# A row-sum kernel: closing barriers under the last store, and another order of waits

## The chip, the cores and the metric

The kernel runs on one core of a Trainium2 chip. The time is device microseconds (us) of one execution. Beside it stands the span: from the first to the last instruction of the program in the profile. The time is longer than the span; the difference is called the *rest* here.

A ratio is the mean time of one kernel's fast runs over that of the kernel before in the same rounds, so not quite the ratio of the medians quoted beside it. Spans of single runs are known to 0.1 us; a mean rest over four or five runs is therefore good to about 0.03 us.

## The reference

```python
batch, seq, dim = 32, 512, 1024          # x: float32, 64 MiB
def reference(x, divisor):               # divisor = 1024.0
    return (np.sum(x, axis=-1) / divisor).astype(np.float32)
```

That is 16,384 rows of 1,024 numbers, each summed and divided.

## The kernel before

Each of the 128 partitions holds 128 rows. SyncE (SP) issues large loads, three buffers in turn. VectorE (DVE) sums most rows of a buffer in one reduction, and ScalarE (ACT) takes some. The last eight rows per partition come in ever smaller pieces; the last row is cut into `pa`, `pb` and `pc`, so that little work is left when the last bytes land. Of the kernel's body only the end is shown here; the comments are added:

```python
    load(pa, x_last[:, L - 1, :a])
    load(pb, x_last[:, L - 1, a:b])
    load(pc[:, : D - b], x_last[:, L - 1, b:])

    nc.gpsimd.tensor_scalar_mul(out=res, in0=res, scalar1=scale)
    tc.keep_in_program_order(nc.sync.dma_start(out=o_main, in_=res))     # 60 KB

    act_sum(pc[:, D - b : D - b + 1], pa)
    nc.vector.reduce_sum(out=pc[:, D - b + 1 :], in_=pb, axis=AX)        # L124
    nc.vector.reduce_sum(out=q[:, L - 1 :], in_=pc, axis=AX)             # L125
    nc.vector.scalar_tensor_tensor(out=fin, in0=q, scalar=scale, in1=r, op0=MULT, op1=ADD)   # L126
    tc.keep_in_program_order(nc.sync.dma_start(out=o_last, in_=fin))     # L127, 4 KB
```

Behind this the framework closes the program (L158 in the profile). Two words for what follows: a *semaphore* is a counter that instructions and transfers change and that an instruction can wait on; a *drain* is an instruction of an engine's sequencer with which, here, an engine closes its work and joins a barrier. SyncE waits for everything that is still under way, the last store included. Then all five engines meet in a first barrier, GpSimd clears the program's semaphores, and they meet in a second barrier.

## Time and profile before

| what | before |
|---|---|
| time, median of 3 runs | 162.98 us |
| span of the profiled run | 161.5 us |
| last piece of input landed | 158.25 us |
| last arithmetic (L126) ended | 159.14 us |
| last store issued / landed | 159.17 / 160.58 us |
| last engine left the second barrier | 161.51 us |

Read it from below: the span ends 3.26 us after the last input byte, and nearly 2.4 us of that lie behind the last arithmetic. The change is about those microseconds alone. To the same end belongs this line of the closing records (duration in ns as min/median/max, first and last start), for the semaphore instructions of SyncE that start between 159.55 and 160.7 us:

```profile
L158 SPq EVENT_SEMAPHORE  x5: 27/28/912, 159.6 to 160.7; - x5
```

Four of the five take 28 ns or less. The fifth, 912 ns, holds the wait for the store to land.

### The profile page before, as it was taken

To read this page: it belongs to the slowest core of one execution; us is meant where nothing else is said; L and a number is where in the kernel's file an instruction comes from. 1 tells how busy PE (TensorE), PEld (TensorE's weight loads), DVE (VectorE), ACT (ScalarE), POOL (GpSimd) and SP (SyncE) were. 2 spreads that over 40 slices of the span, in tenths; PEclk is the share of its full clock that TensorE was granted. 3 is DMA by queue.
4 is the path that set the end of the run, shared out by engine and by line. 5 is a ranking of instruction groups with operands and counts; after the bars stand their busy time and mean duration, and the time that the engine had idled before them with its cause. 6 is when DMAs were issued, how large, how long until landed. Compare 5 with 4: busy or idle time off the path is not lost.

```text
span 161.5 us, 138 instructions
## 1 busy us (share of the span) xinstructions
DVE 120.0 (74%) x15; ACT 20.7 (13%) x39; POOL 0.8 (0%) x6
## 2 busy tenths in 40 slices
DVE  0000099968998699959995999599968970697893
ACT  3000000000000000000000000000008100682881
POOL 0000000000000000000000000000000000000100
DMA  9999999999989999999999899999999978999990
GB/s 298 398 440 454 454 454 454 454 440 440 412 355 398 454 454 454 454 454 454 440 440 412 355 398 454 454 454 454 454 454 440 440 327 383 487 414 394 410 384 6
DMA packets 2448, 67.18 MB, mean 416 GB/s; under 512 B 528, under 2 KB 912, under 8 KB 1040
## 3 DMA queue, kind: packets, MB, share of 16 engines
q1 hardware_dynamic: 2448, 67.18, 97.1%
HBM read 67.11 MB, written 0.07 MB: 416 GB/s over the span
## 4 chain that ended last, share of the span: by engine, by line
DMA 67%; DVE 29%; another core or an unknown queue 1%; SPq 1%; issue 0%; DVEq 0%
DMA t<-in_x_dram 45%; DVE res L87 28%; DMA row<-in_x_dram 22%; SPq L76 1%; DVE q L107 1%; DVE q L125 0%; DVE pc L124 0%; DVE fin L126 0%; DVEq L125 0%; DVEq L126 0%
## 5 line engine op out<-in xcount | busy, mean ns | idle before, releaser
L87 DVE TENSOR_REDUCE res<-t 128x14 f32<-128x14336 f32 (+3 forms) x9 | 114.4, 12716 | 38.2 <-DMA t<-in_x_dram 38.2
L81 ACT ACTIVATE junk<-t 128x1024 f32<-128x1024 f32 x17 | 17.2, 1013 | 135.6 <-DMA t<-in_x_dram 135.6
L87 DVE TENSOR_REDUCE q<-t 128x2 f32<-128x2048 f32 (+1 forms) x2 | 3.5, 1752 | 0.7 <-DMA t<-in_x_dram 0.7
L81 ACT ACTIVATION_READ_ACCUMULATOR junk<-t 128x1 f32 x17 | 3.2, 188 | 0.0
L81 ACT ACT_TABLE_LOAD x1 | 1.3, 1283 | 1.7 <-PEq L144 1.7
L120 POOL TENSOR_SCALAR res<-res 128x120 f32<-128x120 f32 x1 | 0.5, 513 | 151.0 <-DVE res L87 151.0
L107 DVE TENSOR_REDUCE q<-row 128x1 f32<-128x768 f32 x1 | 1.0, 953 | 0.1
L125 DVE TENSOR_REDUCE q<-pc 128x1 f32<-128x322 f32 x1 | 0.5, 489 | 0.1
L81 ACT ACTIVATE junk<-pa 128x448 f32<-128x448 f32 x1 | 0.5, 547 | 0.1
L124 DVE TENSOR_REDUCE pc<-pb 128x1 f32<-128x256 f32 x1 | 0.4, 420 | 0.0
L81 ACT ACTIVATE junk<-row 128x256 f32<-128x256 f32 x1 | 0.4, 388 | 0.2 <-DMA row<-in_x_dram 0.2
L126 DVE SCALAR_TENSOR_TENSOR fin<-q,r 128x8 f32<-128x8 f32 x1 | 0.2, 167 | 0.1
L81 ACT ACTIVATION_READ_ACCUMULATOR junk<-row 128x1 f32 x1 | 0.2, 188 | 0.0
L81 ACT ACTIVATION_READ_ACCUMULATOR junk<-pa 128x1 f32 x1 | 0.2, 185 | 0.0
L73 POOL MEMSET r<- 128x8 f32 x1 | 0.1, 105 | 1.3 <-POOLq L144 1.3
L144 POOL MEMSET const-bfloat16-1.0<- 128x1 bf16 x1 | 0.1, 102 | 0.0
L144 POOL MEMSET const-uint8-127<- 128x1 uint8 x1 | 0.1, 102 | 0.0
L144 POOL MEMSET const-float32-0.0<- 128x1 f32 x1 | 0.1, 99 | 0.2 <-issue 0.2
L144 POOL MEMSET const-float32-1.0<- 128x1 f32 x1 | 0.1, 100 | 0.0
## 6 DMA issues: line engine op xcount, KB each, us to landing
t<-in_x_dram SPq DMA_DIRECT2D x8, 7168.0 KB, 35.7
t<-in_x_dram SPq DMA_DIRECT2D x1, 4096.0 KB, 28.5
t<-in_x_dram SPq DMA_DIRECT2D x1, 2048.0 KB, 33.0
t<-in_x_dram SPq DMA_DIRECT2D x1, 1024.0 KB, 35.0
row<-in_x_dram SPq DMA_DIRECT2D x1, 512.0 KB, 35.9
pa<-in_x_dram SPq DMA_DIRECT2D x1, 224.0 KB, 36.0
pc<-in_x_dram SPq DMA_DIRECT2D x1, 160.0 KB, 35.7
pb<-in_x_dram SPq DMA_DIRECT2D x1, 128.0 KB, 35.8
```

What stands on the lines that cost most here:

```text
L73: nc.gpsimd.memset(r, 0.0)
L76: tc.keep_in_program_order(nc.sync.dma_start(out=dst, in_=src))
L81: nc.scalar.activation(junk[:, :n], src, COPY, scale=by, accum_out=dst)
L87: nc.vector.reduce_sum(out=dst[:, :d], in_=t[:, :d, :], axis=AX)
L107: nc.vector.reduce_sum(out=q[:, j : j + 1], in_=row[:, :c], axis=AX)
L120: nc.gpsimd.tensor_scalar_mul(out=res, in0=res, scalar1=scale)
L124: nc.vector.reduce_sum(out=pc[:, D - b + 1 :], in_=pb, axis=AX)
L125: nc.vector.reduce_sum(out=q[:, L - 1 :], in_=pc, axis=AX)
L126: nc.vector.scalar_tensor_tensor(out=fin, in0=q, scalar=scale, in1=r, op0=MULT, op1=ADD)
L144: nc = _bacc.Bacc("TRN2", target_bir_lowering=False, num_devices=1)
```

## The change

There are two parts. `close_while_storing` takes the last store out of the body and puts it behind SyncE's first closing drain, gives it a semaphore of its own (`landed`), and puts the wait for that semaphore behind both barriers. `latest_wait_first` sorts the waits of an instruction that has several. An instruction carries one wait itself (the *embedded* one, the first of the list); the others become separate semaphore instructions ahead of it on the engine's sequencer.

```diff
+def latest_wait_first(nc):
+    def rank(i, w):
+        own = {"DVE": "DVE_", "Activation": "Activation_", "SP": "DVE_", "Pool": "DVE_"}
+        if w.ant_name.startswith("DMAHW") and i.engine != SP:
+            return 0
+        return 1 if w.ant_name.startswith(own.get(str(i.engine).split(".")[-1], "?")) else 2
+    ...   # sorts on_wait of each body instruction by rank
+
+def close_while_storing(nc, landed):
+    ...   # drain: SyncE's first closing drain, without the waits for the store and for L126
+    last = nc.sync.wait_ge(landed, 16).ins
+    body.instructions = [i for i in body.instructions if i.name != store.name]
+    end.instructions = [
+        with_sync(drain, on_wait=tuple(needs.values())),
+        with_sync(store, on_wait=(done,), on_update=(add,)),
+        *end.instructions[1:-1],
+        with_sync(last, on_update=(sub,)),
+    ]
...
+    landed = nc.alloc_semaphore("landed")
     nc.at_finalize(start_loads_at_once)
+    nc.at_finalize(latest_wait_first)
+    nc.at_finalize(lambda nc: close_while_storing(nc, landed))
```

## The prediction

> **What bounds the kernel now.** I read the page first, for the limit of the bulk, then the chain of waits for the last microseconds, and then the records of the closing barrier, since the change touches only the end and the order of waits.
>
> The page's slices (the program's 161.5 us in 40 pieces; busy tenths of the DMA engines, and the rate):
>
> ```profile
> DMA  9999999999989999999999899999999978999990
> GB/s 298 398 440 454 454 454 454 454 440 440 412 355 398 454 454 454 454 454 454 440 440 412 355 398 454 454 454 454 454 454 440 440 327 383 487 414 394 410 384 6
> ```
>
> The 16 DMA engines are busy from the first slice to the last but one: the kernel reads 67.11 MB and is bound by that. The view by stretches says the same: from 10 to 120 us the DMA share is 1.00 at 434 GB/s, while VectorE is busy for 90.5 of those 110 us. The last piece of the input (`pc`) is issued at 122.52 and lands at 158.25 us by its record. Nothing before that can be moved by this change: it touches no load and no buffer.
>
> What follows is a serial tail. The chain of waits (start, us, what), its last lines:
>
> ```profile
> 121.04 35.86 DMA row<-in_x_dram
> 156.90 0.02 issue
> 156.93 0.95 DVE q L107
> 157.88 0.42 DVE pc L124
> 158.30 0.04 DVEq L125
> 158.33 0.05 issue
> 158.38 0.50 DVE q L125
> 158.88 0.03 issue
> 158.91 0.02 DVEq L126
> 158.93 0.04 issue
> 158.98 0.17 DVE fin L126
> ```
>
> The reader is to see two kinds of step. Between the landing of `row` and L107 there is 0.02 us: that wait is inside the instruction. Before L125 and L126 stands a `DVEq` piece with "issue" around it: a separate semaphore instruction on VectorE's sequencer waits first, and only then is the reduction handed to the engine. L124 to L125 costs 0.10 us so, and L125 to L126 0.10 us (158.87 to 158.98).
>
> The chain stops at the last arithmetic, 159.15 us; the span ends at 161.5. The missing 2.36 us are in SyncE's waits (us in total, times, longest), the issue table (KB, us to landing) and the records of the program's closing line (duration ns min/median/max, first and last start):
>
> ```profile
> SPq L158 <- DMA out_dram<-fin: 0.9, 1, 0.9
> SPq L158 <- PEq L158: 0.6, 2, 0.4
> ...
> out_dram<-fin SPq DMA_DIRECT2D x1, 4.0 KB, 1.4
> ...
> L158 SPq EVENT_SEMAPHORE  x7: 17/28/912, 159.6 to 161.4; - x7
> L158 SPq DRAIN  x3: 7/7/7, 160.8 to 161.1; - x3
> L158 POOLq EVENT_SEMAPHORE_RANGE_CLEAR  x1: 95/95/95, 161.1 to 161.1; - x1
> L158 PEldq EVENT_SEMAPHORE  x2: 51/51/51, 161.0 to 161.5; - x2
> ```
>
> The 4 KB store is issued at 159.17 and lands 1.41 us later, at 160.58. SyncE spends that time in one semaphore instruction of 912 ns. Only then do the two closing barriers run, with GpSimd's clearing of the semaphores between them. By the records, SyncE's drain that joins the first barrier starts at 160.82, and the last release of the second ends at 161.51. So from the landing to the end pass 0.93 us: 0.24 us in which SyncE works off its remaining semaphore instructions and its first drain, and 0.69 us of barriers.
>
> **What the Trainium skill says.**
> - "Perfetto Trace Analysis", section "DMA Instruction — HWDGE (DVE, Sync)": the reported slice of a DMA is its issue alone; the data movement lies outside, and the semaphore write behind a write to HBM can be late. The trace agrees: the store's slice is 0.34 us, its landing 1.41 us after the start.
> - The same page, section "DVE / Act Engine Instruction (TENSOR_ADD, Activation, etc)": an instruction is pushed into a wait queue and waits there, while the sequencer decodes on; a semaphore instruction is the sequencer's own work. The trace agrees: 0.02 us from landing to start with the wait inside, 0.10 us from one reduction's end to the next with a separate wait between.
> - "DMA: Bandwidth & Descriptors", section "Rules for kernel authors": to overlap a DMA with other work, issue it early and wait on its semaphore late. Here the store can't go earlier, but the other work, the barriers, can go under its flight.
> - "Runtime: NRT & Kernel Launch", section "The ~15µs preamble/postamble breakdown": behind the kernel follow a barrier that waits for all engines, and resets. The trace ends before that; I see only that the time (162.98) is 1.48 us over the span (161.5), and take this rest as unchanged.
>
> **The change part by part.**
>
> 1. *The store leaves the body and goes behind SyncE's first closing drain.* That drain keeps its other waits: all loads, the 60 KB store of `res`, GpSimd, ScalarE. It drops VectorE's last count, which the store now waits for itself. The latest of the kept ones is the `res` store, landed at 158.51 by its record. The drain's separate waits come at 0.06 us each (159.56, 159.63, 159.69 in the trace), five at most, so SyncE is through by about 158.7 and stands at the store well before `fin` is ready at 159.1. **Cost 0.**
>
> 2. *The barriers run while the store flies.* After its issue (0.34 us) SyncE goes to the barrier. In the trace the next instruction comes 0.05 us after the issue, and a drain right behind three issued loads took 0.125 us with those loads in flight for tens of us: a drain does not wait for transfers. So the barriers start some 0.4 to 0.55 us after the start of the issue, take 0.69 us, and end 1.1 to 1.25 us after it. The landing comes at 1.41. **The barriers fit under the flight, with 0.15 to 0.3 us to spare.**
>
> 3. *One wait is added at the very end*, on the store's own semaphore, with a subtraction of 16 in the same instruction. A semaphore instruction starts within 0.02 us of its semaphore and takes 17 to 28 ns: **0.04 us** after the landing. I take it that the store has its own semaphore so that the clearing between the barriers does not wipe a count that is still arriving. So the 0.93 us from landing to end become 0.04: **saves 0.89 us.**
>
> 4. *The order of waits.* The sort puts a load's wait first outside SyncE, then VectorE's own on VectorE, ScalarE's own on ScalarE, and VectorE's for GpSimd. I read "first" as the embedded one, after the function's name; no trace of the kernel before can show that. What it moves:
>  - L126 (`fin`): VectorE's own wait becomes embedded; the separate one is for the old zeroing of `r` and long met. 0.10 us become some 0.03 (the store starts 0.027 us after L126's end with such a wait): **saves 0.07 us**, on the chain.
>  - L125: the load of `pc` (landed 158.25) becomes embedded, while VectorE's own wait on L124 (ends 158.29) stays separate. The later one is still the separate one, so **I expect 0 here**, within 0.02 either way.
>  - ScalarE's first activation of a tile: the load's separate wait costs it 0.08 us (row: landing 156.90, start 157.01). It gets some 0.06 back, but its last sum is ready at 158.25, before L124 ends: off the chain, **0**.
>  - GpSimd's scaling of `res` starts some 0.1 us earlier, and so its store; that sits behind `pc` on the same queue and lands 0.65 us before `fin` is stored: **0**.
>  - SyncE's load issues already had VectorE's wait inside: **0**.
>
> Sum: 0.89 + 0.07 = 0.96 us. 162.98 - 0.96 = **162.0 us**, which is 0.6% less.
>
> **The rivals.**
> - *The barriers outlast the flight*, or a drain on SyncE does wait for the store. In the first case the end is set by the barriers, 1.25 us or more after the issue; the flight varies, so this costs a tenth or two. In the second the change is worth 0.07 us or a bit more, some 162.8. For it speaks only that the drain behind the loads took 0.125 us instead of 0.007; against it, that the loads were far from landed.
> - *A small store lands later when the barrier traffic runs beside it*, or the first store in the new place takes longer: the flight of 1.41 us is one sample. The store of `res`, 5.1 us, was queued behind loads and tells nothing. 0.2 us more would give 162.2.
> - *The time outside the span grows.* SyncE now arrives alone and last at whatever the runtime does afterwards; if some of it was hidden before, the gain shrinks to about half: 162.5. Equally the other engines may get ahead with it, and the gain grows a little, 161.8.
> - *The bulk swamps it.* The three runs before spread over 0.33 us, a third of the expected gain. A chip with another DMA rate would shift all by more.
>
> **Range and chances.** The middle is 162.0, and I put it at 162.05 for the rivals that eat at the gain. Low: all of the sum, 0.1 us more outside the span, and a run 0.3 us to the good: 161.6. High: half the gain lost: 162.5. 2% is 3.26 us, more than the whole tail after the last arithmetic (2.36 us), so faster by over 2% is nearly excluded, and nothing added on the path is longer than 0.1 us.
>
> **What the profile of the changed kernel would show.** The 912 ns wait is gone; SyncE's barrier drains stand about 0.4 to 0.5 us after the start of the store's issue; the clearing of the semaphores comes before the landing; the last record is SyncE's wait, within 0.05 us of the landing; the span is about 160.5 us. L125 to L126 shrinks from 0.10 to 0.03 us, L124 to L125 stays. The slices of the bulk stay. I am wrong if the barriers only start at the landing, if the store flies over 1.7 us, or if the span falls by 1 us and the time does not.

## The result, and the profile after

The changed kernel took **161.82 us** (median of 4 runs, 161.77 to 161.92) against 162.94 for the kernel before (4 runs): ratio 0.9931, 95% interval 0.9914 to 0.9948. That is 1.12 us or 0.7% less. The output is correct.

The lines of the source moved: L124 to L127 are now L190 to L193, and the program's closing line is L224. The end of the chain of waits of the changed kernel (start, us, what):

```profile
120.83 35.86 DMA row<-in_x_dram
156.70 0.02 issue
156.72 0.95 DVE q L173
157.67 0.40 DVE pc L190
158.08 0.04 DVEq L191
158.11 0.05 issue
158.16 0.50 DVE q L191
158.66 0.02 issue
158.68 0.17 DVE fin L192
```

The `DVEq` piece before the last instruction has gone: `fin` starts 0.035 us after L191 ends, where it was 0.104. The one before L191 is still there: 0.095 us, as before.

The records of the closing line, and of the new last wait (L88):

```profile
L224 SPq EVENT_SEMAPHORE  x7: 17/28/28, 156.7 to 160.0; - x7
L224 SPq DRAIN  x3: 7/7/130, 158.4 to 159.6; - x3
...
L224 PEldq EVENT_SEMAPHORE  x2: 51/51/51, 159.6 to 160.0; - x2
L224 POOLq EVENT_SEMAPHORE_RANGE_CLEAR  x1: 95/95/95, 159.7 to 159.7; - x1
```

```profile
L88 SPq EVENT_SEMAPHORE  x1: 17/17/17, 160.3 to 160.3; - x1
```

None of SyncE's semaphore instructions in these records takes over 28 ns any more: the 912 ns wait is gone. The clearing starts at 159.7 us, and the barriers are over at 160.09, before the store lands at 160.29. SyncE's last wait ends 0.034 us after that landing, and there the span ends, at 160.33.

Two things don't fit so neatly. The span fell by 1.18 us, of which only 0.955 lie behind the last landing of input (3.258 us from that landing to the span's end before, 2.303 after). And the rest fell too: mean time minus mean span is 1.56 us over the four runs of the changed kernel, while the kernel before shows 1.77 to 1.80 in every set of runs below. The prediction had taken the rest as unchanged. The experiments ask about both.

### The profile page after: what moved, and what is told of

Same layout as the page of the kernel before. It is cut to its first block, busy times and chain, and to the rows that moved or that the text cites. A ratio compares the mean times of both kernels' runs of the same rounds, so it can differ in the third digit from the quotient of the medians.

```text
span 160.3 us, 138 instructions
## 1 busy us (share of the span) xinstructions
DVE 119.9 (75%) x15; ACT 20.7 (13%) x39; POOL 0.8 (1%) x6
## 4 chain that ended last, share of the span: by engine, by line
DMA 67%; DVE 30%; another core or an unknown queue 1%; SPq 1%; issue 0%; DVEq 0%
DMA t<-in_x_dram 45%; DVE res L153 28%; DMA row<-in_x_dram 22%; SPq L142 1%; DVE q L173 1%; DVE q L191 0%; DVE pc L190 0%; DVE fin L192 0%; DVEq L191 0%
## 5 line engine op out<-in xcount | busy, mean ns | idle before, releaser
L191 DVE TENSOR_REDUCE q<-pc 128x1 f32<-128x322 f32 x1 | 0.5, 487 | 0.1
L190 DVE TENSOR_REDUCE pc<-pb 128x1 f32<-128x256 f32 x1 | 0.4, 420 | 0.0
```

## The experiments

Four kernels were run at a time on the same chip, in rounds with the kernel before; the three sets ran on different chips. All results were correct. "Tail" is the time from the last landing of input to the span's end in the profile, read from the records of the trace.

### The kernel before against itself

No edit.

> The kernel before, unaltered, against itself. Theory (the 0.2 us by which the changed kernel's loads landed earlier in its profile is chance, not the change): ratio 1.000, interval within 0.002, and the landing of the first load differs between two profiles of the same program by some 0.1 to 0.2 us (19.90 us in the first profile). Rival (the loads of the changed program really start earlier): here the first load lands at 19.90 within 0.03 us, as before. The time outside the span (time minus span) tells what is normal for this program: 1.5 to 1.8 us.

Measured: 163.01 us against 163.01, ratio 0.9999 (0.9981 to 1.0017). The rest was 1.78 us, the tail 3.263. The chain's piece that ends in the landing of the second load, in this second profile of the same program:

```profile
0.43 36.14 DMA t<-in_x_dram
```

In the first profile of the kernel before it was

```profile
0.43 36.37 DMA t<-in_x_dram
```

So loads of one and the same program land 0.23 us apart in two profiles. In the changed kernel's profile that piece is 36.18 us long, between the two. The earlier landing that its trace shows needs no cause in the change, and tails are compared from here on, not spans of single profiles.

### Only the store and the barriers

```diff
-    nc.at_finalize(latest_wait_first)
```

> Only the store behind the first closing drain with its own semaphore; the order of waits as before. Theory (the barriers under the flight carry nearly all): saves 0.89 us against the kernel before, ratio 0.9945; from the landing of the last input piece to the end of the span 2.37 us (3.26 before, 2.30 with the whole change). Rival (both parts matter alike): ratio 0.997.

Measured: 161.93 us against 163.01, ratio 0.9936 (0.992 to 0.9953). The tail is 2.361 us, 0.90 less than the 3.26 of the kernel before, where 0.89 was expected. The time fell by 1.08 us all the same, and the rest is 1.56. This part carries nearly all of the gain, and the fall of the rest belongs to it.

### Only the order of waits

```diff
-    landed = nc.alloc_semaphore("landed")
-    nc.at_finalize(lambda nc: close_while_storing(nc, landed))
```

> Only the order of waits; the store and the closing drain as before. Theory: L126 starts 0.03 us after L125 in place of 0.10, L125 unchanged, so 0.07 us less: ratio 0.9995, not to be told from 1 by the times, but the tail from the landing of the last input piece to the end of the span falls from 3.26 to 3.19 us. Rival (the order carries the 0.16 us that the time fell beyond the 0.96 of the sum): ratio 0.9985.

Measured: 163.01 us, ratio 0.9998 (0.9983 to 1.0013); rest 1.80. The tail is 3.186 us, 0.07 to 0.08 less than before. L126 starts 0.034 us after L125 in place of 0.104, and L125 starts 0.095 us after L124 in place of 0.096. The mechanism and its size are as expected; the times can't show so little.

### The whole change again

No edit of the changed kernel; run in the set above, and once more in the last set.

> The whole change again. Theory: 0.96 us less than the kernel before, ratio 0.9941; tail from the last landing to the end 2.30 us; the first load lands anywhere between 19.6 and 20.0 us. Rival 1 (the change also starts the loads earlier): again 19.69 us and a ratio of 0.993. Rival 2 (the time outside the span shrinks, because four engines leave 0.25 us before SyncE): time minus span about 1.55 us here against 1.7 for the kernel before.

Measured: 161.85 us, ratio 0.9926 (0.9911 to 0.9942), tail 2.311, rest 1.56. So the second rival is right: the time outside the span really shrinks, by 0.21 us. It was this term that made the gain 1.1 us and not 0.96.

### SyncE ends later, the others don't

```diff
+    more = [nc.sync.wait_ge(landed, 0).ins for _ in range(20)]    # become ten instructions
...
-        *end.instructions[1:-1],
+        *end.instructions[1 : -1 - len(more)],
         with_sync(last, on_update=(sub,)),
+        *more,
```

> The whole change, and ten semaphore instructions more (each 0.06 us, long met) on SyncE behind its last wait; the other four engines end as in the changed kernel. The span grows by 0.6 us to about 160.9. Theory A (the time is the span's end plus a fixed rest of 1.56 us): time 162.45, ratio to the kernel before 0.9965. Theory B (the rest counts from the end of the other engines, 1.77 us behind them, and SyncE's end is hidden under it): time about 161.85 to 161.9, ratio 0.993, and time minus span falls to about 1.0.

Measured: 162.15 us against 162.96, ratio 0.995 (0.9937 to 0.9964). The span of the profiled run is 160.8, and the rest fell to 1.34. The last records of TensorE's queue and of the added instructions:

```profile
L226 PEldq EVENT_SEMAPHORE  x1: 51/51/51, 159.9 to 159.9; - x1
```

```profile
L88 SPq EVENT_SEMAPHORE  x10: 28/28/28, 160.3 to 160.8; - x10
```

The other engines were done by 159.97 us, SyncE 0.87 us later. Neither theory holds: A wanted 0.6 us more than the changed kernel, B nothing, and it was 0.3 (162.15 against its 161.85, which is from the set before; 0.35 when each is taken against the kernel before of its own set). Part of SyncE's delay was free.

### All engines leave later

```diff
         with_sync(store, on_wait=(done,), on_update=(add,)),
-        *end.instructions[1:-1],
+        *more,                                                    # the same ten
+        *end.instructions[1 : -1 - len(more)],
```

> The whole change, and the ten semaphore instructions between the store's issue and the drain that joins the first barrier, so that all engines leave 0.62 us later and SyncE's wait for the landing is already met. The span grows by 0.62 minus the slack of 0.25 us, to about 160.65. Theory A (span plus fixed rest): time 0.37 us over the changed kernel, 162.2, ratio 0.995. Theory B (the other engines' end counts): 0.62 us over it, 162.47, ratio 0.9967, and time minus span back at 1.77.

Measured: 162.22 us, ratio 0.9953 (0.9941 to 0.9966), rest 1.73. The barriers moved by less than thought, because SyncE's drain changed. In this kernel its three drains are

```profile
L226 SPq DRAIN  x3: 7/7/7, 158.2 to 160.0; - x3
```

while the changed kernel's list has one of 130 ns. Directly behind the store's issue the drain that joins the barrier takes 130 ns; 0.66 us after the end of that issue, 7 ns, with the store still in flight. So the other engines left 0.49 us later relative to the store's issue (1.700 us after it in place of 1.212), not 0.62. The time rose by 0.37 against the 161.85 of the changed kernel in the set before (by 0.42 when each is taken against the kernel before of its own set). By itself this fits theory A with its 0.37; but the rest went back to 1.73, which A does not allow. The span rose by only some 0.28 (1.732 us from the store's issue in place of 1.448).

### All engines leave a little later

The same with 6 waits, which become three instructions.

> The same with three semaphore instructions (0.19 us), fewer than the slack between the barriers' end and the landing. The span stays at 160.3. Theory A: time as the changed kernel, 161.85. Theory B: 0.19 us over it, 162.04, with a time minus span of 1.75.

Measured: 161.93 us, ratio 0.9932 (0.992 to 0.9945), rest 1.62. For the reason just seen (the drain took 7 ns here too, 0.24 us after the end of the issue) the other engines left only 0.06 us later (1.274 us after the store's issue). The time is 0.08 over that of the changed kernel in another set (0.13 when each is taken against the kernel before of its own set): too little to decide between the theories alone. The span kept its length behind the store's issue (1.446 us), and the rest rose by the 0.06.

### A theory that fits all of these

Take the rest, and add the time by which SyncE ended after the other four engines in the profile. That is the time from the other engines' end to the end of the measurement:

| run | SyncE ends after the others | rest | sum |
|---|---|---|---|
| kernel before (again) | 0 | 1.78 | 1.78 |
| the same ten instructions before the barriers | 0.03 | 1.73 | 1.76 |
| three instructions before the barriers | 0.17 | 1.62 | 1.79 |
| the change without the order | 0.23 | 1.56 | 1.79 |
| the whole change | 0.24 | 1.56 | 1.80 |
| ten instructions at SyncE's end | 0.87 | 1.34 | 2.21 |

The sum is 1.78 us within 0.02 in all rows but the last, where SyncE is far behind; there 1.34 us follow SyncE's own end. Theory C is therefore: *the time ends 1.78 us after the other engines or 1.34 us after SyncE, whichever is later.* In the changed kernel it is the others, and SyncE, which may end 1.78 - 1.34 = 0.44 us after them, ends 0.24 us after them: 0.2 us to spare. Then the landing of the store, which ends the span, does not set the time; the barriers do. The last four runs were made to test that.

### SyncE ends a little later

As for the ten instructions at SyncE's end, with 4 waits, which become two instructions.

> The whole change, with two more semaphore instructions (0.13 us) on SyncE behind its last wait. Theory C, formed from the runs so far: the time is the later of the other engines' end plus 1.77 us and SyncE's end plus 1.34 us; in the changed kernel SyncE then has some 0.2 us to spare, so the time stays at that of the changed kernel in the same rounds (within 0.05 us) while the span grows by 0.13. Theory A (span plus a fixed rest): 0.13 us over it.

Measured: 161.85 us against 161.81 for the changed kernel in the same rounds. The span's end moved to 0.183 us after the landing, from 0.034; the median time moved by 0.04, within the spread of the runs (161.67 to 161.99). The rest fell to 1.41; with 0.38 for SyncE's lead the sum is 1.79. SyncE's end was hidden, as theory C said and A did not.

### The barriers end earlier, the landing stays

SyncE's drain joins the first barrier before the store. The store then must not wait on a semaphore that GpSimd clears meanwhile, so L126 raises a semaphore of the kernel's own, `ready`, instead of VectorE's counter.

```diff
+    ready = nc.alloc_semaphore("ready")          # raised by L126 in place of VectorE's counter
...
         with_sync(drain, on_wait=tuple(needs.values())),
-        with_sync(store, on_wait=(done,), on_update=(add,)),
-        *end.instructions[1:-1],
+        *end.instructions[1 : join + 1],         # up to SyncE's drain of the first barrier
+        with_sync(store, on_wait=(ready_wait,), on_update=(add,)),
+        *end.instructions[join + 1 : -2],
+        with_sync(used, on_update=(down,)),      # wait for ready, take it back to 0
         with_sync(last, on_update=(sub,)),
```

> The whole change, but SyncE's drain joins the first barrier ahead of the store, which waits for the last VectorE instruction on a semaphore of its own that the clearing leaves alone. The barriers then run from VectorE's end on and finish some 0.4 us earlier; landing and SyncE's end stay, so the span stays at 160.3. Theory C: the time falls until SyncE's end counts, by 0.2 us, to 161.65 (span plus 1.34). Theory A and the prediction's own step (the landing sets the end, the barriers lie under the flight): no change, 161.85.

Measured: **161.70 us** (4 runs) against 161.81 for the changed kernel and 163.01 for the kernel before; ratio to the latter 0.9916 (0.9903 to 0.993). TensorE's last record and SyncE's last wait:

```profile
L236 PEldq EVENT_SEMAPHORE  x2: 51/51/51, 159.1 to 159.6; - x2
```

```profile
L97 SPq EVENT_SEMAPHORE  x1: 17/17/17, 160.3 to 160.3; - x1
```

The other engines leave at 159.63 us, 0.73 us after the store's issue in place of 1.21, and SyncE's end is where it was. The tail is 2.305 us, as long as in the changed kernel, and the rest is 1.33, the limit that the ten late instructions had shown. The mean span is even 0.06 us longer than that of the changed kernel beside it (160.32 and 160.26), and the time is shorter. The two kernels' times do not overlap (161.52 to 161.73 against 161.79 to 161.84). The fall is 0.11 us by the medians and 0.15 by the means, where theory C wanted 0.2. A kernel whose last instruction in the trace stands no earlier takes less time: the landing alone can't have set the end before.

### VectorE's own wait first

```diff
-        if w.ant_name.startswith("DMAHW") and i.engine != SP:
+        if w.ant_name.startswith("DMAHW") and i.engine not in (SP, mybir.EngineType.DVE):
```

> The whole change, but on VectorE its own wait goes before a load's, so that L125 embeds the wait on L124 and the load of pc and ScalarE's sum become the separate ones. Theory: L125 starts 0.03 us after L124 in place of 0.095, unless the separate wait for pc, which lands only some 0.04 us before L124 ends, is itself the later one once it has cost its 0.07 us; then 0.05 us. Gain 0.04 to 0.07 us on the changed kernel (ratio to before 0.9925). Rival: the separate waits for pc take the place of the own one, gain 0.

Measured, on the changed kernel: 161.72 us, ratio 0.9922 (0.991 to 0.9935). The end of its chain:

```profile
157.58 0.43 DVE pc L190
158.02 0.04 issue
158.06 0.50 DVE q L191
158.56 0.02 issue
158.58 0.17 DVE fin L192
```

L191 starts 0.057 us after L190 ends, in place of 0.095. It does not get to 0.035, because `pc` lands 0.07 us before L190's end, and the separate wait for it is over only 0.007 us after that end. So it is the separate wait that comes last again, by less. The tail is 2.287 us; the changed kernel's three profiles have 2.289 to 2.311.

> The same, with VectorE's own wait embedded in L125 as well: another 0.04 us less in the tail, which ends in SyncE's end either way. Theory C: 161.61, ratio to the kernel before 0.9915; the fastest version of this study.

Measured, together with the early join: **161.50 us** (4 runs), ratio 0.9907 (0.9893 to 0.992), the fastest version here: 1.5 us less than before, of which 0.3 beyond the change. The gap before L125's place is 0.070 us this time, so this order is worth 0.02 to 0.04 at that place. The time fell by 0.20 against the early join alone. The tail shows no more than 0.02 of that (2.289 against 2.305); the last input landed 0.12 us earlier in its profile, which is inside the spread that two profiles of one program showed. Whether this order of waits also moves the loads, or chance did, is open.

### The changed kernel in the last set

> The changed kernel once more, as the measure for the other three on this chip: 161.85, ratio 0.993, time minus span 1.56.

Measured: 161.81 us, ratio 0.9926 (0.9913 to 0.9938), rest 1.55.

### Behind the span, in the traces already taken

The views of the profile stop at the end of the span. The packed traces hold semaphore updates behind it, which no view prints; they were read for all 14 profiles. Behind the span semaphore 2 is updated nine times, most other semaphores once, then semaphore 2 nine times more. The sixth update of the second nine stands within 0.01 us of the time measured for the profiled run, in all 14 (161.875 us against 161.87 in the changed kernel).

The first four updates come at the same distances behind the other engines' exit in every profile: the first 0.235 us, the fourth 0.518. The fifth follows at 0.54 us. Only in the three kernels in which SyncE ended 0.7 to 0.9 us after the others does it come later, 0.12 to 0.13 us behind SyncE's own end. From the sixth update to the one that gives the time it is 1.145 to 1.148 us in all 14. So the time stands 1.785 us behind the others' exit in eleven profiles and 1.31 to 1.32 us behind SyncE's in the other three. That is theory C, read from the trace and without rounded spans.

The stretch from the last landing of input to the update that gives the time, in one profile each unless two or three are named, leaves out the chance in the loads:

| run | us |
|---|---|
| kernel before (two profiles) | 5.04, 5.05 |
| only the order of waits | 4.97 |
| only the store and the barriers | 3.91 |
| the whole change (three profiles) | 3.85, 3.86, 3.85 |
| ten instructions before the barriers / three | 4.33 / 3.90 |
| ten instructions at SyncE's end / two | 4.27 / 3.84 |
| VectorE's own wait first | 3.84 |
| early join / with VectorE's own wait first | 3.63 / 3.61 |

The change is worth 1.19 us so, the early join 0.22 us beyond it, and SyncE's long delay costs 0.4 us.

## Why the prediction was right, and where a step of it was not

The time on record was 162.05 us, and it came out at 161.82, inside the range.

**Step 1, the store's new place.** Right: SyncE stood at the store in time. Its drain with the kept waits ended at 158.37 us, and `fin` was ready at 158.85.

**Step 2, the barriers fit under the flight.** Right in every number. The joining drain started 0.40 us after the store's issue; the others left 1.21 us after it (predicted: 1.1 to 1.25); the landing came at 1.414 (predicted: 1.41). The rival in which a drain waits for the store fell: it took 130 ns and was over 0.89 us before the landing. The rival in which the store flies longer beside the barriers fell as well: the flight was 1.404 to 1.414 us in all profiles, with the barriers beside it or without.

**Step 3, the added wait.** Right for the span: 0.034 us from landing to end, where 0.04 was expected and 0.93 had been. For the time it was the wrong quantity to ask about. The early join shows that the landing was not what the time waited for. That the sum came so near is in part luck: it counts the 0.89 us by which the end moved behind the landing, while the time hangs on the other engines' exit, which moved by 1.13 us.

**Step 4, the order of waits.** Right: 0.07 us at `fin`, nothing at L125, because the wait that comes last there (VectorE's own) stays the separate one. The description of the change, that the last one is embedded, does not hold for that instruction.

**The term that failed** is in the paragraph on the Trainium skill, where the prediction says of the 1.48 us over the span that it takes "this rest as unchanged". It fell by 0.21 us, from 1.77 to 1.56. (The 1.48 itself set a median against the span of one other run; run by run it was 1.77 to 1.80. And that the trace ends before the runtime's part holds for the views alone: the semaphore updates behind the span are in it.) The tail fell by 0.955 us, against the 0.96 of the sum; with the 0.21 that makes 1.17, and the runs on the same chip show 1.16 (163.01 less 161.85). The prediction had named this as a possibility, "the other engines may get ahead with it, and the gain grows a little, 161.8", but gave it less weight than its opposite: it moved its middle from 162.0 up to 162.05.

What the runs show in place of that step: the time counts from the exit of the other four engines, plus 1.78 us, as long as SyncE is not over 0.44 us behind them. The change let those four leave 1.13 us earlier relative to the store's issue (2.338 us after it before, 1.212 after). With the 0.07 of step 4 that is 1.20 us, near the 1.12 to 1.20 that the times show and the 1.19 of the stretch from the last landing. Which of the four counts is open: they leave within 0.09 us of each other, at the same distances in every profile. What the updates behind the span belong to, beyond their order, is not shown here either.

## What to carry to other kernels

A wait for the last transfer need not stand before the program's closing barriers: let the other engines leave under the flight, on a semaphore that the closing doesn't clear. Then look at every engine's exit, not at the last instruction of the span alone, since an engine that leaves last may still be hidden. And in an instruction with several waits, find by the trace which is met last, and embed that one; a rule by kind of wait misses cases, as at L125.

## What the Trainium skill lacked or had wrong

- "Runtime: NRT & Kernel Launch", section "The ~15µs preamble/postamble breakdown", says that a barrier behind the kernel waits for all engines. It does not say that engines may arrive apart at no cost: SyncE ended 0.24 to 0.38 us after the others without lengthening the time (161.81 and 161.85 us), and 0.87 us after them cost 0.3 to 0.4.
- "Perfetto Trace Analysis", section "Sequencer-only Instruction (DRAIN, etc)", shows a drain's execution as one stage and does not say that its length can depend on what stands before it. On SyncE it took 130 ns directly behind the issue of a store and 7 ns when it came 0.2 or 0.7 us after the end of that issue; in no case did it wait for the transfer.
- I found no page with the price of a separate wait against an embedded one. Here VectorE's next instruction started 0.104 us after the one it depended on with a separate wait, and 0.034 with an embedded one.
